# Log-softmax backward on one core: pairs of groups loaded and stored together, longer runs for half of y, half of the row sums on ScalarE

## The chip, the cores and the metric

The kernel runs on one core of one Trainium2 chip. The metric is device time in microseconds (us), the median of several runs; lower is better. A run counts as slow when it is over 1.5% above the fastest run of the same kernel, and as fast otherwise.

Three engines and the DMA matter here: VectorE (DVE in the profile), ScalarE (ACT), SyncE (SP, which only issues transfers) and 16 DMA engines, which in this kernel move everything between HBM (the chip's main memory) and the on-chip memory.

## The reference

```python
# y and dy: [8, 1024, 8192] float32; y is the log of a softmax over rows of 8192, so exp(y) is small
def reference(y, dy):
    softmax_x = np.exp(y)
    sum_dy = np.sum(dy, axis=-1, keepdims=True)
    return (dy - softmax_x * sum_dy).astype(np.float32)
```

Two arrays are read and one is written, 268.44 MB each. 8192 rows make 32 groups of 256 rows; a group puts two rows in each of 128 partitions. So one group of dy, y or the output is 8 MiB, 64 KiB per partition, and those 64 KiB are contiguous in HBM.

## The kernel before

```python
R = 2                                   # rows per partition
G = N // (P * R)                        # 32 groups
dyp = tile_pool(name="dyp", bufs=2)     # 2 x 64 KiB per partition
yp = tile_pool(name="yp", bufs=R)       # 2 x 32 KiB
# ... (views y_v, dy_v, out_v: [g, p, (r d)])

def load_dy(g):
    dy_t = dyp.tile([P, R * D], fp32, name="dy_t")
    nc.sync.dma_start(out=dy_t[:], in_=dy_v[g])
    s_t = stats.tile([P, R], fp32, name="s_t")
    nc.vector.tensor_reduce(out=s_t[:], in_=dy_t[:].rearrange("p (r d) -> p r d", r=R),
                            axis=mybir.AxisListType.X, op=ALU.add, negate=True)
    return dy_t, s_t

def load_y(g):                          # by rows: two loads in 32 KiB runs
    for r in range(R): ...
        nc.sync.dma_start(out=y_t[:], in_=y_v[g][:, r * D : (r + 1) * D])

def compute(dy_t, s_t, y_ts):           # in two pieces of 4096 per row, in place
    ...
    nc.scalar.activation(e, e, EXP)
    nc.vector.scalar_tensor_tensor(out=d, in0=e, scalar=s_t[:, r : r + 1], in1=d,
                                   op0=ALU.mult, op1=ALU.add)

cur = load_dy(0)
for g in range(G):
    y_ts = load_y(g)
    compute(*cur, y_ts)
    nxt = load_dy(g + 1)
    store(g, cur[0])                    # one store of 8 MiB
    cur = nxt
    # ... (the last two groups: their stores are put at the end)
```

## Time and profile before

| | before |
|---|---|
| median of the runs known when the prediction was made | 1871.92 us (1868.21 to 1875.18) |
| profiled span | 1865.4 us |
| DMA queue: share of 16 engines, rate | 99.9%, 432 GB/s |
| DVE busy / ACT busy | 1119.2 us / 457.1 us |

These are lines of the page of the kernel before. In the first part a line gives busy time, share of the span and instructions. The DMA row gives the busy share of the DMA engines in tenths, in 40 slices of the span. The queue line gives packets, MB and the packets' time as a share of 16 engines' span. Then come the chain of waits and three groups of instructions, with busy time, mean ns of one, and the idle time before them.

```profile
DVE 1119.2 (60%) x160; ACT 457.1 (25%) x129; POOL 0.2 (0%) x4
DMA  9999999999999999999999999999999999999999
q1 hardware_dynamic: 18576, 805.31, 99.9%
DMA 74%; DVE 17%; ACT 6%; SPq 1%; issue 1%; DVEq 0%; ACTq 0%
L70 DVE SCALAR_TENSOR_TENSOR dy_t<-y_t,s_t,dy_t 128x4096 f32<-128x4096 f32 x128 | 568.1, 4481 | 490.3 <-ACT y_t L69 490.1
L69 ACT ACTIVATE y_t<-y_t 128x4096 f32<-128x4096 f32 x128 | 455.9, 3608 | 1375.6 <-DMA y_t<-in_y_dram 1375.6
L47 DVE TENSOR_REDUCE s_t<-dy_t 128x2 f32<-128x16384 f32 x32 | 551.0, 17220 | 232.1 <-DMA dy_t<-in_dy_dram 232.1
```

The DMA engines have packets in hand for 99.9% of the span. The two compute engines wait, ScalarE for y. The chain passes through DVE and ACT for 23% of the span. The timeline of one period of the kernel before (start, duration in us, engine, line, operation):

```profile
113.31 0.34 SPq L77 DMA_DIRECT2D out_dram<-dy_t  x1
113.75 0.86 SPq L60 DMA_DIRECT2D y_t<-in_y_dram  x2
120.33 17.22 DVE L47 TENSOR_REDUCE s_t<-dy_t 128x2 f32<-128x16384 f32 x1 [7.04 <-DMA dy_t<-in_dy_dram]
139.66 0.33 SPq L45 DMA_DIRECT2D dy_t<-in_dy_dram  x1
...
162.75 8.88 DVE L70 SCALAR_TENSOR_TENSOR dy_t<-y_t,s_t,dy_t 128x4096 f32<-128x4096 f32 x2 [0.83 <-ACT y_t L69]
171.66 0.34 SPq L77 DMA_DIRECT2D out_dram<-dy_t  x1
```

The store issued at 113.31 has to wait for DVE's last instruction of its group, so it is on the chain. But when it is issued, the load of the next dy is still running: it lands at 120.33, where the reduction starts. The DMA engines have 7 us of work left. The period here is 58.15 us (the next issue of dy, 139.66, against 197.81 us one period on); the median over the run is 58.08 us.

The trace also records every DMA packet. Nearly all packets of 64 KiB take 2418 ns and those of 32 KiB 1213 ns, to within 10 ns (98% of them in this kernel). I call this their usual time; the sum over all packets at their usual time, divided by 16, is the least time that the transfers need at that rate, 1859.1 us for this kernel. What the packets took above it, also divided by 16, is called slow-packet time; it is 4.0 us here.

### The profile page before, as it was taken

The numbers are of one execution on the slowest core, as the hardware profiler recorded it, in microseconds if no ns is written. First come the engines' busy times: TensorE is split into PE (matmuls) and PEld (weight loads), VectorE is DVE, ScalarE is ACT, GpSimd is POOL, SyncE is SP. The second block draws the span as 40 slices with busy tenths as digits, with TensorE's granted clock in tenths as the row PEclk, the third lists the DMA queues.
The fourth block names the chain that finished last, engine by engine and source line by source line (L and its number), as shares of the span: only waits on it lengthen the run. The fifth ranks groups of instructions, "written<-read, shape, count | busy, mean of one in ns | idle before, by whom it ended". The sixth has DMA issues, their size and how long they took to land.

```text
span 1865.4 us, 712 instructions
## 1 busy us (share of the span) xinstructions
DVE 1119.2 (60%) x160; ACT 457.1 (25%) x129; POOL 0.2 (0%) x4
## 2 busy tenths in 40 slices
DVE  5675555755557555575555755657656576565664
ACT  2123321233212332123321233212332113331132
POOL 0000000000000000000000000000000000000000
DMA  9999999999999999999999999999999999999999
GB/s 427 416 434 431 443 433 422 435 437 436 427 433 431 440 430 434 431 429 441 433 437 425 433 442 431 434 425 436 438 434 433 428 434 437 437 431 430 429 435 396
DMA packets 18582, 805.36 MB, mean 432 GB/s; under 512 B 2064, under 2 KB 2064, under 8 KB 2064
## 3 DMA queue, kind: packets, MB, share of 16 engines
q1 hardware_dynamic: 18576, 805.31, 99.9%
q14 instruction: 6, 0.05, 0.0%
HBM read 536.87 MB, written 268.44 MB: 432 GB/s over the span
## 4 chain that ended last, share of the span: by engine, by line
DMA 74%; DVE 17%; ACT 6%; SPq 1%; issue 1%; DVEq 0%; ACTq 0%
DMA y_t<-in_y_dram 69%; DVE dy_t L70 15%; ACT y_t L69 6%; DMA dy_t<-in_dy_dram 3%; DVE s_t L47 2%; DMA out_dram<-dy_t 1%; SPq L60 1%; SPq L77 1%; DVEq L122 0%; ACTq L69 0%; DVEq L70 0%
## 5 line engine op out<-in xcount | busy, mean ns | idle before, releaser
L70 DVE SCALAR_TENSOR_TENSOR dy_t<-y_t,s_t,dy_t 128x4096 f32<-128x4096 f32 x128 | 568.1, 4481 | 490.3 <-ACT y_t L69 490.1
L69 ACT ACTIVATE y_t<-y_t 128x4096 f32<-128x4096 f32 x128 | 455.9, 3608 | 1375.6 <-DMA y_t<-in_y_dram 1375.6
L47 DVE TENSOR_REDUCE s_t<-dy_t 128x2 f32<-128x16384 f32 x32 | 551.0, 17220 | 232.1 <-DMA dy_t<-in_dy_dram 232.1
L69 ACT ACT_TABLE_LOAD x1 | 1.3, 1283 | 0.7 <-PEq L111 0.7
L111 POOL MEMSET const-bfloat16-1.0<- 128x1 bf16 x1 | 0.1, 102 | 0.0
L111 POOL MEMSET const-uint8-127<- 128x1 uint8 x1 | 0.1, 102 | 0.0
L111 POOL MEMSET const-float32-1.0<- 128x1 f32 x1 | 0.1, 99 | 0.0
L111 POOL MEMSET const-float32-0.0<- 128x1 f32 x1 | 0.1, 98 | 0.2 <-issue 0.2
## 6 DMA issues: line engine op xcount, KB each, us to landing
y_t<-in_y_dram SPq DMA_DIRECT2D x64, 4096.0 KB, 35.9
out_dram<-dy_t SPq DMA_DIRECT2D x2, 4096.0 KB, 22.6
dy_t<-in_dy_dram SPq DMA_DIRECT2D x32, 38.7
out_dram<-dy_t SPq DMA_DIRECT2D x31, 26.1
```

Source lines behind the costliest of these rows:

```text
L47: nc.vector.tensor_reduce(out=s_t[:], in_=dy_t[:].rearrange("p (r d) -> p r d", r=R), axis=mybir.AxisListType.X, op=ALU.add, negate=True,)
L60: nc.sync.dma_start(out=y_t[:], in_=y_v[g][:, r * D : (r + 1) * D])
L69: nc.scalar.activation(e, e, EXP)
L70: nc.vector.scalar_tensor_tensor(out=d, in0=e, scalar=s_t[:, r : r + 1], in1=d, op0=ALU.mult, op1=ALU.add)
L77: nc.sync.dma_start(out=out_v[g][:, k * w : (k + 1) * w], in_=dy_t[:, k * w : (k + 1) * w])
L111: nc = _bacc.Bacc("TRN2", target_bir_lowering=False, num_devices=1)
```

## The change

The intent: keep the bytes, but (1) load two groups and then store two, so that the direction changes half as often; (2) load y of the first group of a pair in one piece, in 64 KiB runs, and y of the second by rows; (3) let ScalarE sum every second row of dy, with an accumulating copy, so that DVE has half the reductions. The buffers are two of 64 KiB for dy and one of 64 KiB for y, the same as before; new is `copied`, 16 KiB per partition of PSUM (a second on-chip memory), into which ScalarE's copies are thrown away. The compute goes in three pieces per row instead of two. The core of the diff:

```diff
-        nc.vector.tensor_reduce(
-            out=s_t[:],
-            in_=dy_t[:].rearrange("p (r d) -> p r d", r=R),
+        nc.vector.tensor_reduce(
+            out=s_t[:, 0:1], in_=x[:, :D], axis=mybir.AxisListType.X, op=ALU.add, negate=True
         )
+        for h in range(2):
+            nc.scalar.activation(
+                copied[:], x[:, D + h * H : D + (h + 1) * H], COPY, accum_out=half_t[:, h : h + 1]
+            )
+        nc.vector.tensor_scalar( ... )       # cut: -(half 0 + half 1)
...
+    PIECES = [(0, 2048), (2048, 5120), (5120, D)]    # compute in three pieces per row
...
-    cur = load_dy(0)
-    for g in range(G):
-        ...
+    for g in range(0, G, 2):
+        load_dy(g, x_ts[0])
+        load_y(g, 0, W)
+        s_t = sums(x_ts[0])
+        for r in range(R):
+            compute(x_ts[0], s_t, r)
+        load_dy(g + 1, x_ts[1])
+        s_t = sums(x_ts[1])
+        for r in range(R):
+            load_y(g + 1, r * D, (r + 1) * D)
+            compute(x_ts[1], s_t, r)
+        for j in range(2):
+            nc.sync.dma_start(out=out_v[g + j], in_=x_ts[j][:])
```

The order of the instructions on SP is: dy, y, dy, y row, y row, store, store, and so on.

More of the change, by code (lines that the diff above doesn't have):

```diff
@@ L10 @@
 EXP = mybir.ActivationFunctionType.Exp
+COPY = mybir.ActivationFunctionType.Copy
 ALU = mybir.AluOpType
@@ L30 @@
     R = 2
+    W = R * D
     G = N // (P * R)
-    assert N == G * P * R
-    CD = D // 2
+    assert N == G * P * R and D == 8192 and G % 2 == 0
+    H = D // 2
+    PIECES = [(0, 2048), (2048, 5120), (5120, D)]
     y_v = y.flatten_outer_dims().rearrange("(g p r) d -> g p (r d)", p=P, r=R)
@@ L37 @@
     out_v = out.flatten_outer_dims().rearrange("(g p r) d -> g p (r d)", p=P, r=R)
-    dyp = ctx.enter_context(tc.tile_pool(name="dyp", bufs=2))
-    yp = ctx.enter_context(tc.tile_pool(name="yp", bufs=R))
-    stats = ctx.enter_context(tc.tile_pool(name="stats", bufs=2))
-    def load_dy(g):
-        dy_t = dyp.tile([P, R * D], fp32, name="dy_t")
-        nc.sync.dma_start(out=dy_t[:], in_=dy_v[g])
+    pool = ctx.enter_context(tc.tile_pool(name="pool", bufs=1))
+    stats = ctx.enter_context(tc.tile_pool(name="stats", bufs=3))
@@ L46, in load_dy, with sums @@
+    psum = ctx.enter_context(tc.tile_pool(name="psum", bufs=1, space=bass.MemoryType.PSUM))
+    x_ts = [pool.tile([P, W], fp32, name=f"x{j}") for j in range(2)]
+    y_t = pool.tile([P, W], fp32, name="y_t")
+    copied = psum.tile([P, H], fp32, name="copied")
+    def load_dy(g, x):
+        nc.sync.dma_start(out=x[:], in_=dy_v[g])
+    def sums(x):
         s_t = stats.tile([P, R], fp32, name="s_t")
+        half_t = stats.tile([P, 2], fp32, name="half_t")
         nc.vector.tensor_reduce(
-            out=s_t[:],
@@ L49, in load_dy @@
-            in_=dy_t[:].rearrange("p (r d) -> p r d", r=R),
-            axis=mybir.AxisListType.X,
-            op=ALU.add,
-            negate=True,
-        )
-        return dy_t, s_t
-    def load_y(g):
-        y_ts = []
-        for r in range(R):
-            y_t = yp.tile([P, D], fp32, name="y_t")
-            nc.sync.dma_start(out=y_t[:], in_=y_v[g][:, r * D : (r + 1) * D])
-            y_ts.append(y_t)
-        return y_ts
-    def compute(dy_t, s_t, y_ts):
-        for r in range(R):
-            for c in range(0, D, CD):
-                e = y_ts[r][:, c : c + CD]
-                d = dy_t[:, r * D + c : r * D + c + CD]
-                nc.scalar.activation(e, e, EXP)
-                nc.vector.scalar_tensor_tensor(
-                    out=d, in0=e, scalar=s_t[:, r : r + 1], in1=d, op0=ALU.mult, op1=ALU.add
-                )
@@ L74, in store @@
-    def store(g, dy_t, parts=1):
-        w = R * D // parts
-        for k in range(parts):
-            nc.sync.dma_start(
-                out=out_v[g][:, k * w : (k + 1) * w], in_=dy_t[:, k * w : (k + 1) * w]
-            )
-    cur = load_dy(0)
-    for g in range(G):
-        if g < G - 1:
-            y_ts = load_y(g)
-            compute(*cur, y_ts)
-            nxt = load_dy(g + 1)
-            if g < G - 2:
-                store(g, cur[0])
-                cur = nxt
-            else:
-                held, cur = cur, nxt
-        else:
-            y_ts = load_y(g)
-            compute(*cur, y_ts)
-            store(g - 1, held[0])
-            store(g, cur[0], parts=R)
+            out=s_t[:, 0:1], in_=x[:, :D], axis=mybir.AxisListType.X, op=ALU.add, negate=True
+        )
@@ new lines, in sums, with load_y @@
+        for h in range(2):
+            nc.scalar.activation(
+                copied[:], x[:, D + h * H : D + (h + 1) * H], COPY, accum_out=half_t[:, h : h + 1]
+            )
+        nc.vector.tensor_scalar(
+            out=s_t[:, 1:2],
+            in0=half_t[:, 0:1],
+            scalar1=half_t[:, 1:2],
+            scalar2=-1.0,
+            op0=ALU.add,
+            op1=ALU.mult,
+        )
+        return s_t
+    def load_y(g, lo, hi):
+        nc.sync.dma_start(out=y_t[:, lo:hi], in_=y_v[g][:, lo:hi])
@@ new lines, in compute @@
+    def compute(x, s_t, r):
+        for b, e in PIECES:
+            cs = slice(r * D + b, r * D + e)
+            nc.scalar.activation(y_t[:, cs], y_t[:, cs], EXP)
+            nc.vector.scalar_tensor_tensor(
+                out=x[:, cs],
+                in0=y_t[:, cs],
+                scalar=s_t[:, r : r + 1],
+                in1=x[:, cs],
+                op0=ALU.mult,
+                op1=ALU.add,
+            )
+    for g in range(0, G, 2):
+        load_dy(g, x_ts[0])
+        load_y(g, 0, W)
+        s_t = sums(x_ts[0])
+        for r in range(R):
+            compute(x_ts[0], s_t, r)
+        load_dy(g + 1, x_ts[1])
+        s_t = sums(x_ts[1])
+        for r in range(R):
+            load_y(g + 1, r * D, (r + 1) * D)
+            compute(x_ts[1], s_t, r)
+        for j in range(2):
+            nc.sync.dma_start(out=out_v[g + j], in_=x_ts[j][:])
```

## The prediction

> **What bounds the kernel now.** The DMA engines, all of the time. The page's slices show DMA at 9 tenths or more throughout; its queue part gives queue q1 99.9% of 16 engines' span: 805.31 MB at 432 GB/s. DVE is busy 1119.2 us (60%), ACT 457.1 us (25%). The chain of waits is 74% DMA, but its 17% DVE and 6% ACT are not exposed: the view by stretches shows DMA share 1.00 and 434 GB/s there too (118 to 176 us). The timeline repeats every 58.08 us, one group of 25.17 MB: 433 GB/s.
>
> The trace's DMA packet records: a 64 KiB packet mostly takes 2418 ns and never less; a 32 KiB packet 1213 ns. That is 8 ns per packet and 27.2 GB/s per engine, 435 GB/s on 16, which agrees with the 435.2 GB/s port ceiling of the Trainium skill ("DMA: Bandwidth & Descriptors", section "Where 436 GB/s comes from"). Loads and stores take the same. All 8064 large and 8448 small packets at their floors make 1859.1 us; of the profiled span of 1865.4 us, about 4 us are packets above the floor, 1.2 us semaphore writes, the rest start and end.
>
> **What the change does.**
> - Bytes: unchanged.
> - Packets: y of every second group goes as 64 KiB runs, 2048 large for 4096 small packets; the final store is not split. 8 ns per packet over 16 engines: 1.1 us less (floor 1858.05 us).
> - Order: two groups loaded, two stored, half as many switches between loading and storing. The packets show no cost at a switch: nothing.
> - DVE: 32 reductions of 17.22 us become about 8.6 us (estimate, half), -275 us busy; three pieces per row instead of two add 10 to 15 us. ACT: 64 copies of about 3.6 us (as the equal-sized exponentials), +230 us. Neither is critical.
>
> **Is a new wait exposed?** By the order of SP's instructions, with estimates from the durations above (19.35 us of DMA per 8 MiB), every transfer is issued in time:
> - y of the second group, row 0, needs row 0 of the first computed, about 11 us after that y landed; the dy load between covers 19.3 us. Row 1: ready at 20 us, needed at 29 us.
> - The second store needs the last row, about 11 us after the last y, under the first store's 19.3 us: 8 us of slack.
> - The next pair's first dy waits for the first store to land; the second store then covers 19.3 us.
> So a pair should take 116.1 us, twice 58.08. The last compute lies under the first of the last two stores, as it does now.
>
> **Prediction.** Nothing that can be told from noise: profiled span about 1864 us; timed, 1870.8 us against 1871.92. Range 1864 to 1878, mainly the scatter of the runs before (1868.21 to 1875.18). Chances: faster by over 2% 0.01, within 2% 0.97, slower by over 2% 0.02. Faster by over 2% needs over 440 GB/s, above the ceiling.
>
> **What would show it.** DMA share 99.9%, 432 to 433 GB/s; 64 KiB packets still at 2418 ns; pair period 116 us; DVE about 860 us, ACT about 690 us; DMA share below 1 only at the ends.
>
> **What would make it wrong.** A bubble at a pair's end, where loads wait for a store's landing, or y for its only buffer: each us per pair is 16 us in all. Or packets above 2418 ns in longer one-way stretches.

## The result

| | before | changed |
|---|---|---|
| median (range) of 6 runs each | 1868.88 us (1867.29 to 1875.18) | 1867.50 us (1866.34 to 1868.11) |
| ratio, 95% interval | | 0.9985 (0.997 to 1.0) |
| profiled span | 1865.4 us | 1865.9 us |
| DVE busy / ACT busy | 1119.2 / 457.1 us | 859.8 / 698.7 us |

A ratio here is the mean time of one kernel's fast runs over that of the other's fast runs of the same rounds, so it is not quite the ratio of the medians. The interval touches 1, and the first runs of the kernel before, the slowest, pull its mean up. Later its median was 1867.5 to 1867.8 us, which leaves no difference to be seen; the changed kernel was not run again.

The same lines of the changed kernel's page (its parts are renamed: x is dy and output, `copied` the throw-away copy of ScalarE's sums):

```profile
DVE 859.8 (46%) x256; ACT 698.7 (37%) x321; POOL 0.2 (0%) x4
DMA  9999999999999999999999999999999999999999
q1 hardware_dynamic: 16128, 805.31, 99.9%
DMA 64%; DVE 13%; ACT 10%; another core or an unknown queue 9%; issue 1%; SPq 0%; DVEq 0%; ACTq 0%
L81 DVE SCALAR_TENSOR_TENSOR x<-y_t,s_t,x 128x3072 f32<-128x3072 f32 (+1 forms) x192 | 579.4, 3059 | 255.7 <-ACT y_t L80 255.7
L57 DVE TENSOR_REDUCE s_t<-x 128x1 f32<-128x8192 f32 x32 | 277.8, 8682 | 722.3 <-DMA x<-in_dy_dram 722.3
L80 ACT ACTIVATE y_t<-y_t 128x3072 f32<-128x3072 f32 (+1 forms) x192 | 460.1, 2466 | 269.4 <-DMA y_t<-in_y_dram 253.2
L61 ACT ACTIVATE copied<-x 128x4096 f32<-128x4096 f32 x64 | 229.6, 3587 | 864.9 <-DMA x<-in_dy_dram 863.9
```

DVE lost 259 us of work and ACT gained 242 us, and the span did not notice. Only the DMA rows count, and they are unchanged: 99.9%, with 2448 fewer packets (272 completion writes included) for the same 805.31 MB. For an instruction with immediate scale and bias, the Trainium skill ("ScalarE: Activation LUTs", section "What ACT_TABLE_LOAD costs") gives 186 ns and 0.833 ns per element; an estimate from it for 4096 elements is 3598 ns. The mean of one copy, for which the kernel names neither scale nor bias, is 3587 ns, which agrees.

The chain now goes 13% through DVE and 10% through ACT ("another core or an unknown queue" is what the view could not assign). That this is again no exposed compute can be read from the end of a pair in the changed kernel's timeline:

```profile
167.12 12.35 DVE x L81 x4
179.85 37.38 DMA out_dram<-x
217.25 38.69 DMA x<-in_dy_dram
```

```profile
197.98 7.22 ACT L80 ACTIVATE y_t<-y_t 128x2048 f32<-128x2048 f32 x3 [2.52 <-DMA y_t<-in_y_dram]
199.93 2.35 DVE L81 SCALAR_TENSOR_TENSOR x<-y_t,s_t,x 128x2048 f32<-128x2048 f32 x1 [0.33 <-ACT y_t L80]
202.58 6.75 DVE L81 SCALAR_TENSOR_TENSOR x<-y_t,s_t,x 128x3072 f32<-128x3072 f32 x2 [0.30 <-ACT y_t L80]
...
217.25 0.34 SPq L52 DMA_DIRECT2D x<-in_dy_dram  x1
217.69 0.76 SPq L75 DMA_DIRECT2D y_t<-in_y_dram  x1
236.89 0.33 SPq L52 DMA_DIRECT2D x<-in_dy_dram  x1
```

The first three lines are from the chain of waits in order of time (start, duration, what). The others are from the timeline. The last y lands at 197.98 us; its row is finished at 209.33 us, and the second store is issued at once. The first store lands at 217.25 us, which is when the next dy, waiting for that buffer, can be issued. So the second store is issued 7.9 us before the first has landed (the prediction said 8), and the next dy 19.6 us before the second has landed (236.89 us). In this stretch the DMA engines always have the next transfer in hand. The view by stretches of the changed kernel shows it for two whole pairs (duration, busy time and count of DVE, ACT and POOL, granted clock, DMA share, GB/s):

```profile
101.00:217.30 116.30, 53.74 (x16) 43.59 (x20) 0.00 (x0) 1.00 1.00 433
217.30:333.80 116.50, 53.74 (x16) 43.59 (x20) 0.00 (x0) 1.00 1.00 432
```

### The profile page after: what moved, and what is told of

Its sections match the earlier page's. It is cut to its first block, busy times and chain, and to the rows that moved or that the text cites. A ratio compares the mean times of both kernels' runs of the same rounds, so it can differ in the third digit from the quotient of the medians.

```text
span 1865.9 us, 923 instructions
## 1 busy us (share of the span) xinstructions
DVE 859.8 (46%) x256; ACT 698.7 (37%) x321; POOL 0.2 (0%) x4
## 3 DMA queue, kind: packets, MB, share of 16 engines
q1 hardware_dynamic: 16128, 805.31, 99.9%
## 4 chain that ended last, share of the span: by engine, by line
DMA 64%; DVE 13%; ACT 10%; another core or an unknown queue 9%; issue 1%; SPq 0%; DVEq 0%; ACTq 0%
DMA x<-in_dy_dram 31%; DMA out_dram<-x 30%; DVE x L81 13%; ACT copied L61 6%; ACT y_t L80 4%; DMA y_t<-in_y_dram 3%; SPq L75 0%; DVEq L128 0%; ACTq L128 0%; SPq L52 0%; ACTq L80 0%; ACTq L61 0%
## 5 line engine op out<-in xcount | busy, mean ns | idle before, releaser
L81 DVE SCALAR_TENSOR_TENSOR x<-y_t,s_t,x 128x3072 f32<-128x3072 f32 (+1 forms) x192 | 579.4, 3059 | 255.7 <-ACT y_t L80 255.7
L57 DVE TENSOR_REDUCE s_t<-x 128x1 f32<-128x8192 f32 x32 | 277.8, 8682 | 722.3 <-DMA x<-in_dy_dram 722.3
L80 ACT ACTIVATE y_t<-y_t 128x3072 f32<-128x3072 f32 (+1 forms) x192 | 460.1, 2466 | 269.4 <-DMA y_t<-in_y_dram 253.2
L61 ACT ACTIVATE copied<-x 128x4096 f32<-128x4096 f32 x64 | 229.6, 3587 | 864.9 <-DMA x<-in_dy_dram 863.9
L61 ACT ACTIVATION_READ_ACCUMULATOR copied<-x 128x1 f32 x64 | 11.9, 186 | 0.0
L64 DVE TENSOR_SCALAR s_t<-half_t 128x1 f32<-128x1 f32 x32 | 6.5, 204 | 0.0
```

What stands on the lines that cost most here:

```text
L57: nc.vector.tensor_reduce(out=s_t[:, 0:1], in_=x[:, :D], axis=mybir.AxisListType.X, op=ALU.add, negate=True)
L61: nc.scalar.activation(copied[:], x[:, D + h * H : D + (h + 1) * H], COPY, accum_out=half_t[:, h : h + 1])
L64: nc.vector.tensor_scalar(out=s_t[:, 1:2], in0=half_t[:, 0:1], scalar1=half_t[:, 1:2], scalar2=-1.0, op0=ALU.add, op1=ALU.mult,)
L80: nc.scalar.activation(y_t[:, cs], y_t[:, cs], EXP)
L81: nc.vector.scalar_tensor_tensor(out=x[:, cs], in0=y_t[:, cs], scalar=s_t[:, r : r + 1], in1=x[:, cs], op0=ALU.mult, op1=ALU.add,)
```

## The experiments

Theory: the DMA engines at their packet rate set the time, and nothing else is exposed. Twelve kernels test it and its rivals. "Idle DMA" below is the complement of the queue's share of the span. Slow-packet time is as defined above, from the packet records.

Comparisons with the changed kernel's time are between calls, which ran on different chips; the kernel before was run in every call, at medians of 1867.5 to 1868.9 us, so the calls can be compared to about 1 us.

A warning about correctness. Two kernels that return dy itself passed the comparison with the reference: exp(y) is so small on this input that the product hardly counts. A pass therefore says that the transfers are right, and little of the arithmetic. All kernels passed but that of experiment 7.

### 1. The transfers of both kernels alone

The changed kernel without compute, and later the kernel before without compute (the diff is that of the first):

```diff
-        s_t = sums(x_ts[0])
-        for r in range(R):
-            compute(x_ts[0], s_t, r)
...
-        s_t = sums(x_ts[1])
...
-            compute(x_ts[1], s_t, r)
```

> The changed kernel with all sums, exponentials and multiply-adds taken away; the same transfers on the same buffers in the same order (output is dy, wrong on purpose). Theory (the DMA engines alone set the time; no wait for compute is exposed): within 0.2% of the changed kernel's 1867.5 us, DMA share 99.9%. Rival (some compute wait is exposed; the chain of waits has 13% DVE and 10% ACT): clearly faster, by up to 23% if the chain is taken literally.

> The kernel before with all compute taken away: the same transfers in the same order (output wrong on purpose), 32 switches where the transfers of the changed kernel have 16. Theory (no exposed compute before, and a switch costs about 0.1 us): 1865 to 1868 us, within 0.2% of the kernel before and 0 to 2 us above the 1865.9 us of the changed kernel's transfers. Rival (the kernel before had a wait for compute that the packets hide): over 0.3% faster than the kernel before.

Measured: the changed kernel's transfers alone 1865.94 us (1865.84 to 1866.53), against 1867.50 us with compute. The transfers of the kernel before took 1867.74 us, ratio 0.9995 (0.9983 to 1.0007). Nearly the whole time is there with no compute at all. The rival that took the chain literally is out for both kernels. This also agrees with the Trainium skill ("SBUF — State Buffer", section "SBUF: two separate sides"), which says that compute accesses and DMA use disjoint ports and can't slow each other: with compute, these two kernels took at most 1.6 us more. (In experiment 8 packets do get slower when DVE's work is changed; what does it stayed open.) What fixes the packet time itself, the engines, a port or the HBM, was not tested: no run varied it.

### 2. Packet size

```diff
+    Q = 512
-    y_t = pool.tile([P, W], fp32, name="y_t")
+    y_t = pool.tile([P, W // Q, Q + 8], fp32, name="y_t")   # padded: each run is 2 KiB
...
-        nc.sync.dma_start(out=y_t[:, lo:hi], in_=y_v[g][:, lo:hi])
+        nc.sync.dma_start(out=y_t[:, lo // Q : hi // Q, :Q], in_=y_v[g][:, lo:hi].rearrange("p (k q) -> p k q", q=Q))
...                                    # cut: compute() goes through the same padded rows
```

> The changed kernel with y loaded in 2 KiB runs (131072 packets for 6144), same bytes and order, the buffer padded. Theory of a fixed 8 ns per packet: 124928 x 8 ns / 16 = 62 us more, 1930 us, ratio about 1.033; a 2 KiB packet takes about 83 ns. Rival (the 8 ns seen between two large sizes does not carry down to small packets): clearly more or less than 62 us. Correct output.

Measured: 1928.54 us, ratio 1.0327 (1.0313 to 1.0341); span 1926.9 us, 61.0 us over the changed kernel's. The cost per added packet is 61.0 us x 16 / 124928 = 7.8 ns. (A 2 KiB packet is recorded at 84 ns most often and 87 ns on the mean, but the records overlap, to 101.6% of the span, so the span is the better measure.) So about 8 ns per packet holds from 64 KiB down to 2 KiB, and the data packets that the change saves, 2048 of y and 128 of the last store, are worth 1.1 us: too little to see, as predicted.

### 3. The longer runs alone, in the kernel before

```diff
-    yp = ctx.enter_context(tc.tile_pool(name="yp", bufs=R))
+    yp = ctx.enter_context(tc.tile_pool(name="yp", bufs=1))
...
-        y_ts = []
-        for r in range(R):
-            y_t = yp.tile([P, D], fp32, name="y_t")
-            nc.sync.dma_start(out=y_t[:], in_=y_v[g][:, r * D : (r + 1) * D])
-            y_ts.append(y_t)
-        return y_ts
+        y_t = yp.tile([P, R * D], fp32, name="y_t")
+        nc.sync.dma_start(out=y_t[:], in_=y_v[g])
+        return [y_t[:, r * D : (r + 1) * D] for r in range(R)]
```

> The kernel before with one change, the packet size: y of every group as one load in 64 KiB runs (4224 large for 8448 small packets). Theory: no new wait, since the next y load stood behind a store that needs the whole group anyway; 8 ns saved for each pair of packets over 16 engines, 2.1 us less, ratio about 0.999. Rival (longer runs load faster, and the gain is lost elsewhere in the changed kernel): over 0.5% faster. Correct output.

Measured: 2004.28 us, ratio 1.0732. This expectation of mine failed: it counted the packets and overlooked a wait. Its queue line and a stretch of its timeline:

```profile
q1 hardware_dynamic: 13968, 805.31, 94.3%
```

```profile
107.93 10.61 ACT L66 ACTIVATE y_t<-y_t 128x4096 f32<-128x4096 f32 x3
108.06 17.67 DVE L67 SCALAR_TENSOR_TENSOR dy_t<-y_t,s_t,dy_t 128x4096 f32<-128x4096 f32 x4 [27.72 <-ACT y_t L66]
125.64 17.21 DVE L47 TENSOR_REDUCE s_t<-dy_t 128x2 f32<-128x16384 f32 x1
125.76 0.34 SPq L74 DMA_DIRECT2D out_dram<-dy_t  x1
```

```profile
124.00:126.00 2.00, 2.00 (x2) 0.00 (x0) 0.00 (x0) 1.00 0.00 0
```

When y comes in one piece, neither row can be started until all of it is there. Then both rows take one exponential and 17.67 us of DVE, about 21 us, and the store that waits for them has only one load of dy (19.35 us) in front of it. DVE goes straight from the last multiply-add to the next sum, without the 7 us wait that it had before: dy had landed already, and nothing was left in the queue. The last line, from the view by stretches, shows it: from 124 to 126 us, round the issue of the store, no packet starts. The DMA engines idle 5.7% of 2002.4 us, 114 us, and slow-packet time is 30 us. So the longer runs can't be had by themselves in the order of before; they need an order that puts more transfers behind the whole y.

### 4. The longer runs for both groups of the pair

```diff
-        for r in range(R):
-            load_y(g + 1, r * D, (r + 1) * D)
-            compute(x_ts[1], s_t, r)
+        load_y(g + 1, 0, W)
+        for r in range(R):
+            compute(x_ts[1], s_t, r)
```

> The changed kernel with y of the second group as one load too. Run lengths alone: 1.0 us less. Theory of exposed waits: y's only buffer is free about 1 us after the second dy has landed (62.3 against 61.4 us in the profile), so with the time from issue to first packet the DMA idles 2 to 3 us there; and both rows are computed after the whole y landed, so the second store is ready about 21 us after it and the first store covers 19.3 us, another 3 us. 5 to 6 us per pair, 80 to 100 us in all, ratio 1.043 to 1.055. Correct output.

Measured: 1995.69 us, ratio 1.0683 (1.0669 to 1.0697), more than expected. DMA idles 4.6% of 1994.3 us, 92 us or 5.7 us per pair, as forecast (5 to 6). The rest, missing from my sum, is slow-packet time: 45 us, against 4.6 us in the changed kernel. Loading y of the second group by rows is what saves the changed kernel from this.

### 5. A second store made late on purpose

```diff
             load_y(g + 1, r * D, (r + 1) * D)
+            if r == 1:
+                for k in range(2):
+                    d_t = stats.tile([P, 1], fp32, name="d_t")
+                    nc.vector.tensor_reduce(out=d_t[:], in_=x_ts[1][:, D:], axis=mybir.AxisListType.X, op=ALU.add)
             compute(x_ts[1], s_t, r)
```

> The changed kernel with two extra reductions of 8.7 us each of the second group's row (results unused), put by the scheduler before each row's multiply-adds. It uses up the slack of the second store: in the profile the last multiply-add ends about 8 us before the first store lands; 17.4 us more, of which some fills DVE's idle time, make it end 6 to 8 us after. Theory: a DMA gap of 7 to 9 us per pair at the first store's end, 110 to 145 us in all, ratio 1.06 to 1.08. Rival (nothing but the bytes matters whatever compute does): same time. Correct output.

Measured: 2001.06 us, ratio 1.0711 (1.0698 to 1.0725), 8.3 us per pair, in the expected range. Of this 6.9 us are idle DMA (5.5% of the span; 7 to 9 were expected) and most of the rest is slow-packet time, 29.7 us in all against 4.6. The DMA row of its page, with dips at the pairs' ends:

```profile
DMA  9989899898998989989899998999989999899998
```

The compute has slack, and the slack has an end. It was read from the profile to about a microsecond.

### 6. Stores on a second queue

```diff
-            nc.sync.dma_start(out=out_v[g + j], in_=x_ts[j][:])
+            nc.scalar.dma_start(out=out_v[g + j], in_=x_ts[j][:])
```

> The changed kernel with the stores issued by ScalarE, a second queue, so that loads and stores are in flight together. Theory (the ceiling is that of the engines, whichever way bytes go): 1865 to 1870 us, ratio 0.998 to 1.002, 433 GB/s. Rival (one queue serialises the two directions and a mix of them could go beyond 435 GB/s): over 1% faster. A slowdown of a few per cent would mean that ScalarE's wait for the store's data delays its exponentials. Correct output.

Measured: 1980.44 us over six runs with a wide scatter (1953.75 to 2005.27); three of them count as slow, being over 1.5% above the fastest, and the ratio of the three others is 1.0535 (1.0492 to 1.0577). My figure for the theory missed: I had looked at ScalarE's waits and not at what the two queues do to each other's landing times. The rival that two directions at once could pass the ceiling is not borne out; the rate was 413 GB/s, though with gaps, so the ceiling of a mix without gaps was not measured. In the profiled run, which was the fastest of them, the first store shares the engines with the two rows of y and lands together with the last of them (223.3 and 223.1 us), so the next dy can only be issued then, with nothing in flight. DMA idles 2.7% of 1952.0 us, 53 us, and slow-packet time is 40 us. What makes the other runs longer still was not seen, and no weight is put on them.

### 7. One switch instead of 16

```diff
-    for g in range(0, G, 2):
-        ...                               # the whole loop
+    bufs = [x_ts[0], y_t, x_ts[1]]
+    n = 0
+    for g in range(G):
+        for v in (dy_v, y_v):
+            nc.sync.dma_start(out=bufs[n % 3][:], in_=v[g])
+            n += 1
+    for g in range(G):
+        nc.sync.dma_start(out=out_v[g], in_=bufs[g % 3][:])
```

> Transfers only, all in 64 KiB runs: all 64 loads, then all 32 stores (output wrong on purpose), so one switch from loading to storing where the changed kernel has 16 and the kernel before 32. Theory: packets at their floor make 1857.0 us, semaphore writes about 1.2, start and end about 3: 1861 to 1863 us in the profile, 0.2% below the changed kernel, with excess over the floor only at the start and at the one switch. Rival (switches cost much): over 1% faster.

Measured: 1862.90 us, ratio 0.9972 (0.9959 to 0.9985), span 1861.1 us, as the theory had it. The output is wrong. All the switches and all the short runs together are worth 0.3%. The usual time of its packets alone is 1857.0 us, so an order that leaves the packets at their usual time can gain hardly more than that. (Its one switch came when the queue was empty, since the first store waits for the last load, so it doesn't show what a switch with a full queue costs.)

### 8. The order alone, and the parts undone one by one

In the first of these kernels, y of both groups comes by rows and all sums are on DVE, which leaves the new order. The second has only the sums undone, the third only the first y.

```diff
# sums on DVE (first and second kernel)
-        nc.vector.tensor_reduce(out=s_t[:, 0:1], in_=x[:, :D], ...)
-        for h in range(2): ...            # ScalarE's copies and the joining of the halves
+        nc.vector.tensor_reduce(out=s_t[:], in_=x[:].rearrange("p (r d) -> p r d", r=R), ...)
# first y by rows (first and third kernel)
-        load_y(g, 0, W)
+        for r in range(R):
+            load_y(g, r * D, (r + 1) * D)
```

> The changed kernel with y of both groups by rows (32 KiB runs) and all sums on VectorE, so that the order of two groups loaded, two stored is left. Theory: no wait becomes exposed; the packets' floor is within 0.1 us of the kernel before's, half as many switches give at most 1 to 2 us: 1866 to 1869 us, ratio 0.998 to 1.001. Rival (ScalarE's sums are needed to hide compute in the new order): slower by more than 0.5%, with DMA share below 1 at each pair's end. Correct output.

> The changed kernel with one part undone: all sums on VectorE, y of the first group still in one load. It splits the 8 us that the order-only kernel lost, as slow packets round the switches and without idle DMA. Theory S (with the sums on VectorE the second store is issued only 3 us before the first has landed, and a short queue ahead slows the engines): 1872 to 1877 us. Rival R (the first y in two loads of 32 KiB runs did it): 1866 to 1868 us. Both at 1866 to 1868 would mean that it takes both. Correct output.

> The changed kernel with the other part undone: y of the first group by rows, in two loads of 32 KiB runs; sums shared with ScalarE as in the changed kernel. Rival R: 1872 to 1877 us, slow packets at the switches as in the order-only kernel. Theory S: about 1 us over the changed kernel, 1867 to 1869 us. Correct output.

| kernel | median us | ratio (95%) | span us | slow-packet time us |
|---|---|---|---|---|
| changed | 1867.50 | 0.9985 (0.997 to 1.0) | 1865.9 | 4.6 |
| order alone | 1876.02 | 1.0044 (1.0031 to 1.0057) | 1875.3 | 14.2 |
| sums on DVE | 1882.87 | 1.0071 (1.0058 to 1.0085) | 1882.1 | 20.9 |
| first y by rows | 1868.15 | 0.9997 (0.9984 to 1.001) | 1865.7 | 4.2 |

(The ratios are to the kernel before.) The first expectation failed: the order alone was 0.44% slower. The two others vary its parts. With the sums shared, the first y by rows costs nothing that can be seen. With the sums on DVE, about 15 us are lost, more than the theory S of that run allowed for; but neither a gap nor a dip shows. (The order alone has the same sums and y by rows, and lost only about 9 us, so the two parts don't simply add; why is open.) These are the queue line and the DMA row of the kernel with sums on DVE:

```profile
DMA  9999999999999999999999999999999999999999
q1 hardware_dynamic: 16128, 805.31, 99.9%
```

The share is as in the changed kernel, although 16 us were lost. The packets account for it: slow-packet time is 16.3 us more, and the span 16.2 us. They sit in two places of each pair: in the last 32 KiB loads of y before the first store, and in the last packets of the second store before the next dy, up to 1.1 and 0.9 us a time for the 16 engines, 12.7 and 7.0 us in all. In the changed kernel, the same two places cost 0.1 to 0.2 us and almost nothing, but for the first switch of the run, which cost 1.0 us. The timeline of the kernel with sums on DVE shows what is different there:

```profile
883.82 17.20 DVE L55 TENSOR_REDUCE s_t<-x 128x2 f32<-128x16384 f32 x1
...
901.11 17.93 DVE L71 SCALAR_TENSOR_TENSOR x<-y_t,s_t,x 128x2048 f32<-128x2048 f32 x6
...
919.07 0.34 SPq L92 DMA_DIRECT2D out_dram<-x  x1
922.80 0.34 SPq L51 DMA_DIRECT2D x<-in_dy_dram  x1
...
942.12 0.33 SPq L51 DMA_DIRECT2D x<-in_dy_dram  x1
```

```profile
922.80:942.20 19.40, 0.00 (x0) 0.00 (x0) 0.00 (x0) 1.00 0.96 405
```

DVE finishes the pair at 919.04 us and the first store lands at 922.80 us: the second store is issued 3.7 us before that (3.8 on the mean of the pairs), where the changed kernel has 7.9 us. But neither place of slow packets is where this slack is. The slow loads of y in this pair come at 897.6 to 902.0 us, and the first store behind them had been issued at 884.3 us. The slow packets of the second store come from 936.9 us on, with the next dy already issued at 922.80 us, and then no compute runs at all (last line, from the view by stretches: DVE, ACT and POOL have no instruction). So a short queue is not the direct cause in either place, and DVE at work beside the transfers is not in the second; if the late store does it, the effect comes later.

### 9. The same lateness without the long sums

```diff
             load_y(g + 1, r * D, (r + 1) * D)
+            if r == 1:
+                d_t = stats.tile([P, 1], fp32, name="d_t")
+                nc.vector.tensor_reduce(out=d_t[:], in_=x_ts[1][:, :4608], axis=mybir.AxisListType.X, op=ALU.add)
             compute(x_ts[1], s_t, r)
```

> The changed kernel, sums shared with ScalarE as it has them, with one extra reduction of 4608 elements (about 4.9 us, result unused) on VectorE between the second group's rows, so that the second store is issued about 3 us before the first has landed, as in the kernel with all sums on VectorE, but without its 17.2 us reductions. Theory S (a second store issued too shortly ahead makes the switches dear): 1875 to 1885 us, slow packets of 0.5 to 1 us per switch, DMA share still 99.9%. Rival V (VectorE's long reductions beside the transfers slow the packets, whenever the store is issued): 1866 to 1869 us. Correct output.

Measured: 1872.31 us (1869.49 to 1875.66), ratio 1.002 (1.0006 to 1.0034); slow-packet time 10.2 us, DMA share 99.9%. This lies between the two: above what rival V allowed, below what theory S asked for. At one pair in its timeline:

```profile
898.48 4.95 DVE L102 TENSOR_REDUCE d_t<-x 128x1 f32<-128x4608 f32 x1
...
903.34 9.00 DVE L81 SCALAR_TENSOR_TENSOR x<-y_t,s_t,x 128x2048 f32<-128x2048 f32 x3
912.37 0.34 SPq L107 DMA_DIRECT2D out_dram<-x  x1
917.13 0.34 SPq L52 DMA_DIRECT2D x<-in_dy_dram  x1
```

The second store is issued 4.8 us before the first has landed (4.3 on the mean of the pairs), so it came a little less late than planned. After the first switch of the run, slow packets of 0.3 to 0.9 us per switch appear at some pairs, from about 800 us on, and not at others. In this pair they lie at 891.8 to 896.1 us, before the added reduction begins. So the switches got dearer without the 17.2 us reductions. That the late store did it is not shown, because the added reduction came together with it; but the order fits. By the mean time from the issue of the second store to the landing of the first (taken as the issue of the next dy), 7.9 us (changed; first y by rows), 4.3 (this one), 4.2 (order alone) and 3.8 (sums on DVE), the slow-packet time is 4.6 and 4.2, 10.2, 14.2 and 20.9 us. Whether the lateness explains all 15 us of the sums on DVE, or whether something else of DVE's longer sums adds to it, stays open, and so does why a switch gets slow before any gap is to be seen.

No version that computes the result beats both kernels by more than the noise, and experiment 7 shows how little room there is for one.

## Why the prediction was right

- **The transfers bound the kernel; DVE's and ACT's shares of the chain are not exposed.** Shown: the transfers alone take 1867.74 us (before) and 1865.94 us (changed). This is why a change that moves about 250 us of work between engines gained nothing.
- **Ceiling.** Shown as far as it was tried: 433 GB/s at best over a whole run, also with one single switch (1861.1 us), and 413 GB/s with both directions in flight, where there were gaps too.
- **Packets: 1.1 us.** The mechanism holds (7.8 ns per packet down to 2 KiB). The gain itself is below what can be told: by the packet records, the usual time fell from 1859.1 to 1858.05 us and the slow-packet time rose from 4.0 to 4.6 us.
- **No new wait exposed.** Shown: DMA share 1.00 over whole pairs, 7.9 us of slack where 8 were predicted, a pair in 116.3 us against 116.1. With the slack taken away on purpose, 8.3 us per pair appeared (experiment 5).
- **Busy times.** DVE 859.8 us (predicted 860), ACT 698.7 us (690); span 1865.9 us (about 1864). The timed figure, 1870.8 us, was 3.3 us too high because it was reckoned from the first three runs of the kernel before; that it lies in the range is no evidence for the gain of 1.1 us.
- **Two steps were too simple, without harm to the sum.** "The packets show no cost at a switch": they do. Before the switch to the first store, the last loads lose about 1 us once and 0.1 to 0.2 us after that. In the kernel before, the first switches show 0.35 and 0.27 us and most later ones under 0.1 us. And "Neither is critical", said of the sums, is true of the changed kernel and not of the order: with all sums on DVE the slack falls from 7.9 to 3.8 us and 15 us are lost, though the link between the two is not shown. The new order and the longer runs also lean on each other: the whole y alone, in the order of before, costs 137 us by a wait which I overlooked when I wrote the expectation. The change as a whole avoids these costs; it had nothing to gain beyond them.

## What to carry to other kernels

When a profile shows the DMA engines 99.9% busy and most packets at one fixed time, compute the time that the transfers take at that packet time before reordering anything: here it left 0.3% of the span. A rearrangement of such a kernel is judged by slack, which the timeline shows: how long before the queue runs out is each transfer issued, and which compute stands in between. Keep some of it in hand: here the kernels with about 4 us left lost 5 to 15 us in all, for a reason that stayed open, while the DMA share still read 99.9% and the packets got slower.

## What the Trainium skill lacked or had wrong

- "DMA: Bandwidth & Descriptors": its port ceiling of 435.2 GB/s fits the packets (27.2 GB/s per engine without the 8 ns of each packet). The 425 GB/s that it gives as measured, in "Measured", is for one load of 16 MB issued from GpSimd; it has no rate for large transfers in 64 KiB runs, loads and stores, issued from SP. The runs show 432 to 433 GB/s over whole runs.
- The same page, section "Why small descriptors are slow", speaks of a fixed overhead of about 3 cycles per packet and gives no time for it; no page has it in ns for large packets. The runs show 8 ns between 32 and 64 KiB and 7.8 ns down to 2 KiB, for transfers issued from SP.
- No page has the cost of a switch from loading to storing on one queue: after the first switch of the run, 0.1 to 0.2 us for the 16 engines in the changed kernel, and up to 1.1 us in the kernel with all sums on DVE.
- "Perfetto Trace Analysis" warns against the occupancy of the DMA engines as a measure, but not that packets can get slower at a full share: 99.9% at 1865.9 us and at 1882.1 us, for the same bytes and the same packets.
